# A hybrid attention and RWKV layer on one core: the values' channel sum pinned behind the solve

## The chip, the cores and the metric

The kernel runs on one core of a Trainium2 chip. The metric is device time in microseconds, from one launch; of the kernel before there are three timed runs, and one more that was recorded by the profiler. A difference is a change of the median of such runs.

Engines are named as in the profile: PE (matrix), DVE (vector), ACT (scalar), POOL (GpSimd), SP (the queue that issues nearly all DMAs). PEld is PE's loading of stationary operands.

## The reference

One layer, 256 tokens of width 4096, all in float32. One projection of the input feeds 16 heads of attention with forget gates (width 128) and 32 heads of RWKV-7 time mixing (width 64); their outputs are gated, projected and normalised:

```
proj = x @ w_in                                   # fox q,k,v,f | rwkv r,k,v,w,a | gate z
fox  = softmax(q k^T / sqrt(128) + forget decay) v   # causal, per head
rw   = rw + (previous token's rw - rw) * mu       # token shift of r, k, v, w, a
S_t  = S_{t-1} diag(w_t) + (S_{t-1} a_t) b_t^T + v_t k_t^T ;  y_t = S_t r_t
y    = GroupNorm per head(y) + sum(r k r_k) v
out  = LayerNorm(ALPHA * x + (concat(fox, y) * silu(z)) @ w_out)
```

The GroupNorm subtracts each head's mean over its 64 channels. The kernel uses that y is linear in v: it subtracts the mean from the values v, once, before the recurrence. That is the centring of which the change speaks, and the sum over channels is its first step.

## The kernel before

**The main stream.** The projection's weights come in tiles of 512 KB, each holding two of the 32 blocks of 128 input channels by 512 columns. A column block takes 16 such tiles, numbered 0 to 15 (in the profile w_0 to w_15); four column blocks b = 0 to 3 make one pass n, and there are eight passes, one for each pair n of head tiles (128 channels each, two RWKV heads or one attention head). Every tile is split in two halves for float32 accuracy: ACT casts it (line 138, tile w_7h for instance) and DVE subtracts the cast (line 139, w_7l). PE takes three products with them (lines 144 to 146; line 146 is the one that needs the DVE half), four times for each tile. Buffers: four raw tiles, four cast halves, three DVE halves. Then the output projection streams its own tiles in the same way (names wo, lines 784 to 786).

**The side work.** Everything else is done by generators that advance by one step in each `slot()`, two slots for each weight tile. `W` and `LAG` say how many slots each waits between its steps. `chain()` runs `rwkv(n)` for the eight pairs, and around the change it does this, with the block and tile of the stream beside which it stands:

- Block 2: PE multiplies keys and queries of all chunks into four PSUM tiles gp (line 488). POOL turns the values of the pair, which were written to memory and read back one token later (tile vs), into the shifted values: lines 493, 494, 495. POOL also scales the kept keys BK (line 491), once PE has read them. DVE masks gp into gb and lt (lines 506 and 514, eight instructions of 64x512); SP stores parts of gb (line 509) and loads them back in another layout, Nb (line 510).
- Block 2's end to block 3's tile 7: a triangular system is solved by back substitution on DVE, 31 steps of a product (line 536) and a sum (line 539), one step in each slot.
- Behind it, SP stores the solution xc (line 545) and loads it back as T (line 547). DVE sums the values over channels, vm (line 550); eight DVE instructions subtract the mean and write SV (line 557); ACT copies each of the two SV tiles to UV (line 560). Twelve slots later the transposes of T follow (line 566), and the chunk recurrence.

**What sets the order.** The kernel's text is a program order, and a scheduler may place an instruction on its engine ahead of others that it doesn't depend on, when it finds it ready earlier. `tc.keep_in_program_order(...)` takes that freedom from an instruction: it stays behind what stands ahead of it in the text. Lines 537 and 566 pin the solve's first product and the transposes. Line 550 isn't pinned: in the text it stands behind the solve, on DVE it stood in block 2. Each engine takes its instructions strictly in its own order, and waits at the first one that isn't ready.

Of the kernel before, what the change touches and what calls it, by code (L numbers as in the profile page):

```python
# [14 lines left out]
ALU = mybir.AluOpType  # L15
AX = mybir.AxisListType
# [8 lines left out]
HD = 64  # L25
# [57 lines left out]
def layer(ctx: ExitStack, tc: tile.TileContext, xt, xtok, w_lora, w_main, muv, w_o, up, par, mulora, fbias, lng, lnb, cst, out):  # L83
    nc = tc.nc
# [292 lines left out]
    vs_ = {}  # L377
# [98 lines left out]
    def rwkv(n):  # L476
# [12 lines left out]
        v = vv[n]  # L489
        kept = BK[:, :, 0 : NCH - 1, :]  # L490
        nc.gpsimd.tensor_tensor(kept, kept, lc[:, :, 0 : NCH - 1].unsqueeze(3).to_broadcast([P, 2, NCH - 1, P]), ALU.mult)
        p, t = bks[n], vs_[n]
# [54 lines left out]
                nc.sync.dma_start(out=T[B * a : B * (a + 1), u], in_=td[u, a].rearrange("c r s -> r c s"))  # L547
        vm = rp.tile([P, 2, 2, 2], F32, tag="vm", name=f"vm{n}")
        vt = vs_[n].rearrange("p m (u j v) -> p m u j v", u=2, j=2)
        nc.vector.tensor_reduce(vm.rearrange("p m u j -> p (m u j)"), vs_[n].rearrange("p m (a v) -> p (m a) v", v=HD), AX.X, ALU.add)  # L550
        yield
        for j in range(2):
            o = HALF[1 - j]
# [14 lines left out]
        for u in range(2):  # L568
            for c in range(NCH):
                for j in range(2):  # L570
                    a, b = slice(C * j, C * j + B), slice(C * j + B, C * j + C)
# [17 lines left out]
        for u in range(2):  # L589
            for c in range(NCH):  # L590
                for j in range(2):
                    a, b = slice(C * j, C * j + B), slice(C * j + B, C * j + C)
                    nc.tensor.matmul(xp[a, u * P + c * B : u * P + (c + 1) * B], Q[b, u, c, :], X[b, u, c, C * j + B : C * j + C], start=True, stop=True)
        for j in range(2):
            a = slice(C * j, C * j + B)
# [110 lines left out]
    def chain():  # L706
        while not ff:
            yield
        yield from forget()
        for n in range(G // 2):  # L710
            yield from rwkv(n)
# [304 lines left out]
```

## Time and profile before

| what | us |
|---|---|
| timed runs | 1991.75, 1997.97, 1998.69 |
| median | 1997.97 |
| profiled execution, its own time | 1994.46 |
| its span, first to last instruction | 1992.7 |
| PE busy in the span | 1967.0 |
| DVE busy | 1356.3 |
| ACT busy | 999.1 |
| POOL busy | 72.6 |

A row of the timeline has the start, the length, engine, line, operation, the tiles written and read, shapes, how many instructions were merged, and in brackets the idle time of the engine before it with what ended it. A row of the waits has who waited for whom, the total in us, how many times, and the longest. A row of the stretches has its length, the busy time of PE, PEld, DVE, ACT and POOL with the number of instructions, the clock that was granted to PE as a share of the full one, the share of time in which the DMA engines were busy, and GB/s. Matmuls overlap, so a row's length is longer than the spacing from one to the next.

### The profile page before, as it was taken

What the parts mean: (1) busy time and instruction counts of PE and PEld (TensorE: products, weight loads), DVE (VectorE), ACT (ScalarE), POOL (GpSimd) and SP (SyncE); (2) the same over time, 40 slices, a digit from 0 to 9 for tenths busy, and PEclk for the clock granted to TensorE, in tenths of its full rate; (3) what the DMA queues carried; (4) which work ended last, traced back from release to release, by engine and by line L of the source; (5) the groups of instructions that cost most, each with busy time, mean ns of one, the idle gap of its engine ahead of it and who ended that gap; (6) DMA issues with size and microseconds to landing.
All of it is one profiled execution on the core that took longest, in us unless ns stands there. A gap on an engine that the chain in (4) does not pass through costs nothing. (4 is left out here: it accounts for less than half of the span.)

```text
span 1992.7 us, 28327 instructions
## 1 busy us (share of the span) xinstructions
PE 1967.0 (99%) x10377; PEld 1611.1 (81%) x10377; DVE 1356.3 (68%) x2168; ACT 999.1 (50%) x1509; POOL 72.6 (4%) x111
## 2 busy tenths in 40 slices
PE   9999999999999999999999999999999999999998
PEld 7878787878787878787878787877888878888886
DVE  6688577857685767577857785768577856755555
ACT  6554564456445644464446444644465444443332
POOL 0110001000100010001000100010001000000000
PEclk9999999999999999999999999999999999999999
DMA  9556556655666566555655565556555877866664
GB/s 334 159 176 195 182 190 187 198 180 188 179 203 179 191 180 200 181 183 181 206 180 183 182 207 173 191 173 206 182 189 172 266 271 228 256 199 201 195 189 170
DMA packets 146383, 392.86 MB, mean 197 GB/s; under 512 B 32642, under 2 KB 48020, under 8 KB 146244
## 3 DMA queue, kind: packets, MB, share of 16 engines
q1 hardware_dynamic: 145812, 390.63, 62.6%
q8 instruction: 81, 1.33, 0.3%
q14 instruction: 58, 0.48, 0.1%
q10 hardware_dynamic: 432, 0.43, 0.1%
HBM read 374.98 MB, written 16.01 MB: 196 GB/s over the span
## 5 line engine op out<-in xcount | busy, mean ns | idle before, releaser
L138 ACT CAST w_11h<-w 128x1024 fp32r<-128x1024 f32 x31 | 32.6, 1051 | 91.0 <-DMA w<-in_w_main_dram 72.2
L536 DVE TENSOR_TENSOR prod<-Nb,xc 128x8 f32<-128x8 f32 (+30 forms) x248 | 72.5, 292 | 7.1
L539 DVE TENSOR_REDUCE xc<-prod 128x8 f32<-128x16 f32 (+30 forms) x248 | 73.2, 295 | 6.0
L139 DVE TENSOR_TENSOR w_11l<-w,w_11h 128x1024 fp32r<-128x1024 f32 x31 | 37.9, 1223 | 47.0 <-ACT w_11h L138 28.7
L146 PE MATMUL acc<-w_7l,x 128*128 128x512 f32 x124 | 51.8, 418 | 15.4 <-DVE w_7l L139 15.4
L139 DVE TENSOR_TENSOR w_1l<-w,w_1h 128x1024 fp32r<-128x1024 f32 x31 | 37.9, 1224 | 35.7 <-PE acc L146 35.7
L139 DVE TENSOR_TENSOR w_0l<-w,w_0h 128x1024 fp32r<-128x1024 f32 x31 | 37.9, 1224 | 34.0 <-PE acc L146 23.8
L139 DVE TENSOR_TENSOR w_3l<-w,w_3h 128x1024 fp32r<-128x1024 f32 x31 | 37.8, 1221 | 31.8 <-PE acc L146 31.8
L138 ACT CAST w_2h<-w 128x1024 fp32r<-128x1024 f32 x31 | 32.7, 1056 | 52.2 <-PE acc L145 46.8
L138 ACT CAST w_1h<-w 128x1024 fp32r<-128x1024 f32 x31 | 32.7, 1055 | 51.6 <-PE acc L145 42.0
L138 ACT CAST w_0h<-w 128x1024 fp32r<-128x1024 f32 x31 | 32.7, 1056 | 43.5 <-PE acc L145 34.1
L139 DVE TENSOR_TENSOR w_10l<-w,w_10h 128x1024 fp32r<-128x1024 f32 x31 | 38.0, 1225 | 23.6 <-PE acc L146 13.8
L139 DVE TENSOR_TENSOR w_9l<-w,w_9h 128x1024 fp32r<-128x1024 f32 x31 | 37.9, 1224 | 23.0 <-ACT pT L688 19.2
L139 DVE TENSOR_TENSOR w_2l<-w,w_2h 128x1024 fp32r<-128x1024 f32 x31 | 37.9, 1223 | 22.6 <-PE acc L146 22.4
L139 DVE TENSOR_TENSOR w_15l<-w,w_15h 128x1024 fp32r<-128x1024 f32 x31 | 37.9, 1222 | 22.3 <-PE acc L146 20.9
L138 ACT CAST w_13h<-w 128x1024 fp32r<-128x1024 f32 x31 | 32.6, 1053 | 40.7 <-DMA w<-in_w_main_dram 23.8
L144 PE MATMUL acc<-w_4h,x 128*128 128x512 f32 x124 | 53.0, 427 | 0.0
L144 PE MATMUL acc<-w_7h,x 128*128 128x512 f32 x124 | 51.6, 416 | 0.0
L138 ACT CAST w_4h<-w 128x1024 fp32r<-128x1024 f32 x31 | 32.7, 1055 | 36.8 <-PE acc L145 35.5
L144 PE MATMUL acc<-w_6h,x 128*128 128x512 f32 x124 | 51.2, 413 | 0.0
L144 PE MATMUL acc<-w_1h,x 128*128 128x512 f32 x124 | 51.2, 413 | 0.0
L144 PE MATMUL acc<-w_2h,x 128*128 128x512 f32 x124 | 51.1, 412 | 0.0
(836 smaller groups left out, 6582.0 us busy)
## 6 DMA issues: line engine op xcount, KB each, us to landing
w<-in_w_main_dram SPq DMA_DIRECT2D x496, 512.0 KB, 3.5
wo<-in_w_o_dram SPq DMA_DIRECT2D x128, 512.0 KB, 3.6
Nb<-nd SPq DMA_DIRECT2D x16, 512.0 KB, 5.3
wr<-in_w_main_dram SPq DMA_DIRECT2D x15, 512.0 KB, 6.8
hd<-hl SPq DMA_DIRECT2D x29, 256.0 KB, 4.4
h<-hd SPq DMA_DIRECT2D x29, 256.0 KB, 6.6
res<-in_xtok_dram SPq DMA_DIRECT2D x16, 256.0 KB, 4.5
xr<-in_xt_dram SPq DMA_DIRECT2D x15, 256.0 KB, 6.4
```

Of the source, the lines that this page charges most:

```text
L138: nc.scalar.copy(hi[:, :n], src[:, :n])
L139: nc.vector.tensor_tensor(lo[:, :n], src[:, :n], hi[:, :n].bitcast(F32), ALU.subtract)
L144: nc.tensor.matmul(acc[:, :n], xs[k][:, 0, tt], hi[:, o : o + n], start=(k == 0), stop=False)
L146: nc.tensor.matmul(acc[:, :n], xs[k][:, 0, tt], lo[:, o : o + n], start=False, stop=(k == KT - 1))
L536: first = nc.vector.tensor_tensor(prod[:, :, :, s + 1 :], nb[:, :, s : s + 1, s + 1 :].to_broadcast([P, 2, NJ, w]), xc[:, :, :, s + 1 :], ...
L539: nc.vector.tensor_reduce(xc[:, :, :, s : s + 1], prod[:, :, :, s:], AX.X, ALU.add)
```

## The change

Line 550, the sum over the values' channels, is put into `keep_in_program_order`:

```
-        nc.vector.tensor_reduce(vm.rearrange("p m u j -> p (m u j)"), vs_[n].rearrange("p m (a v) -> p (m a) v", v=HD), AX.X, ALU.add)
+        tc.keep_in_program_order(nc.vector.tensor_reduce(vm.rearrange("p m u j -> p (m u j)"), vs_[n].rearrange("p m (a v) -> p (m a) v", v=HD), AX.X, ALU.add))
```

No instruction is added or taken away. The order on PE, POOL and SP is the same; on DVE and ACT three groups move in each of the eight passes. On DVE in block 2 of pair 2, ahead of the masks (vm is the sum, SV_2 the centred values, w_2_5l the DVE half of tile 5 of block 2, gb_838 the first masked tile):

```order
 L266 SCALAR_TENSOR_TENSOR s_4_4972<-tr_1_0_4967,prm,s_4_4972 128x255
 L517 TENSOR_TENSOR bon_4585<-bon_4585,s_4_4972 128x512
-L550 TENSOR_REDUCE vm_5627<-vs_4930 128x8
 L139 TENSOR_TENSOR w_2_5l<-w_2_5_5001,w_2_5h 128x1024
-L557 SCALAR_TENSOR_TENSOR SV_2_5075<-vm_5627,vs_4930 64x2x64 x4
-L557 SCALAR_TENSOR_TENSOR SV_2_5076<-vm_5627,vs_4930 64x2x64 x4
 L139 TENSOR_TENSOR w_2_6l<-w_2_6_5019,w_2_6h 128x1024
 L506 TENSOR_TENSOR gb_838<-gp_0_0_5031,cs 64x512
```

The sum and the eight instructions of the centring have left this place; between the bonus term (line 517) and the masks only the splits of tiles 5 and 6 remain.

On DVE in block 3 of the same pair, at the end of the solve (prod and xc are its last step):

```order
 L536 TENSOR_TENSOR prod_5203<-Nb_5056,xc_5204 128x8x31
 L539 TENSOR_REDUCE xc_5204<-prod_5203 128x8
+L550 TENSOR_REDUCE vm_5627<-vs_4930 128x8
 L139 TENSOR_TENSOR w_3_8l<-w_3_8_5512,w_3_8h 128x1024
+L557 SCALAR_TENSOR_TENSOR SV_2_5075<-vm_5627,vs_4930 64x2x64 x4
+L557 SCALAR_TENSOR_TENSOR SV_2_5076<-vm_5627,vs_4930 64x2x64 x4
 L139 TENSOR_TENSOR w_3_9l<-w_3_9_5540,w_3_9h 128x1024
 L139 TENSOR_TENSOR w_3_10l<-w_3_10_5573,w_3_10h 128x1024
```

They now stand behind the solve's last sum, around the split of tile 8 and ahead of that of tile 9.

On ACT in block 3 of the same pair (UV_2 are the copies of the centred values, pT an attention tile):

```order
 L138 CAST w_3_9h<-w_3_9_5540 128x1024
 L688 COPY pT_5530<-fpt_5526 128x384
+L560 COPY UV_2_5077<-SV_2_5075 64x512
 L138 CAST w_3_10h<-w_3_10_5573 128x1024
+L560 COPY UV_2_5078<-SV_2_5076 64x512
 L138 CAST w_3_11h<-w_3_11_5595 128x1024
 L695 COPY fo_5565<-fop_5562 128x256
```

The two copies followed the centring: from block 2, where they stood around the cast of tile 7, to block 3, around the cast of tile 10.

## The prediction

> **What bounds the kernel now.** I read the page's head first, then what PE waited for, and only then the stretch of one pair of heads in the timeline.
>
> ```profile
> span 1992.7 us, 28327 instructions
> ...
> PE 1967.0 (99%) x10377; PEld 1611.1 (81%) x10377; DVE 1356.3 (68%) x2168; ACT 999.1 (50%) x1509; POOL 72.6 (4%) x111
> ```
>
> PE is the bound: 1967.0 of 1992.7 us. An edit on DVE can only pay by what PE loses to DVE. Of the rows on PE's waits one matters:
>
> ```profile
> PE acc L146 <- DVE w_7l L139: 15.4, 8, 2.1
> ```
>
> Eight waits, one for each pair of heads, all for the same tile: the low half of weight tile 7 in column block 2. The timeline of pair 2 shows why it is late (DVE, then POOL, ACT and PE; columns: start, length):
>
> ```profile
> 530.93 0.69 DVE L550 TENSOR_REDUCE vm<-vs 128x8 f32<-128x512 f32 x1 [4.07 <-POOL vs L495]
> 531.53 1.22 DVE L139 TENSOR_TENSOR w_5l<-w,w_5h 128x1024 fp32r<-128x1024 f32 x1
> 532.78 3.21 DVE L557 SCALAR_TENSOR_TENSOR SV<-vm,vs 64x128 f32<-64x128 f32 x8
> 536.02 1.23 DVE L139 TENSOR_TENSOR w_6l<-w,w_6h 128x1024 fp32r<-128x1024 f32 x1
> 537.17 1.40 DVE L506 TENSOR_TENSOR gb<-gp,cs 64x512 f32<-64x512 f32 x2
> ...
> 542.66 1.21 DVE L139 TENSOR_TENSOR w_7l<-w,w_7h 128x1024 fp32r<-128x1024 f32 x1
> ...
> 533.15 1.47 POOL L491 TENSOR_TENSOR BK<-BK,lc 128x768 f32<-128x768 f32 x1 [2.25 <-PE gp L488]
> ...
> 530.38 1.04 ACT L138 CAST w_6h<-w 128x1024 fp32r<-128x1024 f32 x1
> ...
> 531.22 2.06 PE L488 MATMUL gp<-lt,BK 64*128 64x128 f32 x32
> ...
> 541.18 0.39 PE L144 MATMUL acc<-w_7h,x 128*128 128x512 f32 x1
> 541.41 0.40 PE L145 MATMUL acc<-w_7h,x 128*128 128x512 f32 x1
> 543.92 0.61 PE L146 MATMUL acc<-w_7l,x 128*128 128x512 f32 x1 [2.12 <-DVE w_7l L139]
> ```
>
> DVE stands idle for 4.07 us until POOL has finished the shifted values, takes the sum over channels (L550), the centring (L557), two weight splits, and comes to the eight masks at 537.17, although PE had finished their input at 531.22 + 2.06 = 533.28. The masks run until the split of tile 7 starts at 542.66, which is 5.49 us; the split ends at 543.87 and PE starts at 543.92.
>
> PE loses more than the listed wait. The clock that the throttle granted, in stretches of 3.41 us (columns: length, PE, PEld, DVE, ACT, POOL, clock, DMA share, GB/s):
>
> ```profile
> 144.80:148.21 3.41, 3.41 (x9) 2.63 (x9) 1.98 (x2) 0.00 (x0) 0.00 (x0) 0.50 1.02 245
> 544.16:547.57 3.41, 3.41 (x9) 2.63 (x9) 1.98 (x2) 0.00 (x0) 0.00 (x0) 0.50 0.76 202
> 745.55:748.96 3.41, 3.41 (x10) 2.63 (x9) 1.66 (x3) 0.00 (x0) 0.00 (x0) 0.50 1.00 214
> 1144.91:1148.32 3.41, 3.29 (x8) 2.63 (x9) 2.33 (x3) 0.00 (x0) 0.00 (x0) 0.50 1.05 244
> 344.38:347.79 3.41, 3.41 (x15) 2.81 (x16) 2.95 (x3) 0.00 (x0) 0.00 (x0) 1.00 1.01 237
> 540.75:544.16 3.41, 1.29 (x6) 0.77 (x5) 3.38 (x5) 1.05 (x1) 0.00 (x0) 1.00 0.17 24
> ```
>
> In four of these stretches the clock is 0.50; pair 2's starts at 544.16, right behind the stall that ended at 543.92, and the stretch before it had PE busy for 1.29 of 3.41 us. The other three begin behind the stalls of pairs 0, 3 and 5, and behind pair 1's shorter stall the clock stayed at 1.00. I take it that a stall falling mostly into one such stretch halves the clock for the next.
>
> **What is removed.** Three terms, each eight times or fewer:
> - The listed wait of PE: 15.4 us.
> - Refilling: 541.18 to 541.41 is the regular spacing, 0.23 us; 541.41 to 543.92 is 2.51, so 2.28 is lost where 2.12 is listed. The 0.16 us, eight times: 1.3 us.
> - Half clock: half of 3.41 us in each of four stretches: 4 x 1.7 = 6.8 us.
>
> Sum: 23.5 us. The profiled execution took 1994.46 us (its span and 1.8 us around it), so 1971.0 us, on a span of 1969.2. The median of the three timed runs is 3.5 us above the profiled one; two more half-clock stretches would make that difference (an estimate from the row above, not seen). If it were something else, the sum from the median would be 1974.5. I keep 1971.0, because the changed kernel should have no such stretches left to vary.
>
> **Does the wait go entirely?** In pair 2 the split of tile 6 can start when its ACT half is there, 530.38 + 1.04 = 531.42, and ends at 532.65. The masks then wait for PE until 533.28 at the latest, run 5.49 us to 538.77, and the split of tile 7 ends at 539.98. PE wants it one spacing after 541.41, at 541.64: 1.66 us to spare. The masks now run beside POOL's L491 (1.47 us), which they don't before, and DVE operations do stretch beside POOL:
>
> ```profile
> L557 DVE SCALAR_TENSOR_TENSOR SV<-vm,vs x64: 275/284/1605, 133.1 to 1537.4; 64x128 f32<-64x128 f32 x64
> ```
>
> The median is 0.284 us and the longest 1.605, so the bound for that is 1.605 - 0.284 = 1.32 us, which still leaves 0.34 of the 1.66. The nearer row is that of another operation with one input in PSUM and one in SBUF, as the masks have:
>
> ```profile
> 124.73 0.48 DVE L266 SCALAR_TENSOR_TENSOR s<-tr,prm,s 128x255 f32<-128x255 f32 x1
> ...
> 126.13 0.48 DVE L266 SCALAR_TENSOR_TENSOR s<-tr,prm,s 128x255 f32<-128x255 f32 x1
> ...
> 125.99 1.29 POOL L493 TENSOR_TENSOR vs<-vs,bk 128x512 f32<-128x512 f32 x1 [18.40 <-DMA vs<-vd]
> ```
>
> The second of these runs wholly inside POOL's operation and takes the same 0.48 us. I take zero. A gain beyond the sum is excluded here, since the PE wait can't go below nothing.
>
> **What is added.** The sum, the centring and its two ACT copies now stand in column block 3, behind the solve's last reduce. Pair 2 there, before:
>
> ```profile
> 588.68 0.42 DVE L539 TENSOR_REDUCE xc<-prod 128x8 f32<-128x256 f32 x1
> 589.02 1.22 DVE L139 TENSOR_TENSOR w_8l<-w,w_8h 128x1024 fp32r<-128x1024 f32 x1
> 590.98 1.23 DVE L139 TENSOR_TENSOR w_9l<-w,w_9h 128x1024 fp32r<-128x1024 f32 x1 [0.75 <-issue]
> ...
> 597.31 0.39 PE L146 MATMUL acc<-w_9l,x 128*128 128x512 f32 x1
> ```
>
> New on DVE: 0.69 (L550) + 8 x 0.284 (L557) = 2.96 us ahead of the split of tile 9. Its values have long been ready, so L550 waits for nobody. Of the 2.96 us the idle 0.75 takes the first part; the split then starts at 593.19 and ends at 594.42, and PE wants it at 597.31: 2.9 us to spare. Nothing reaches PE. On ACT the first copy of the centred values (L560) waits for four of the eight pieces, until 589.10 + 0.69 + 1.22 + 4 x 0.284 = 592.15; the casts of tiles 10 and 11 stand behind the two copies. With a copy (64x512 values) at half a cast's 1.04 us (an estimate), tile 10's cast ends near 593.7, ahead of its DVE split, which follows 594.42 anyway. The attention copy and the gate behind them come about 1 us later, which DVE's idle time before tiles 11 and 12 takes up. The solve's result still goes out on SP directly behind L539; L550 stands behind that instruction on DVE, so the round trip through memory isn't held. SP, POOL and PE keep their order. The masks' stores are issued earlier, so the solve's input and the weights behind them on SP come no later than now. I take all this at zero; from below it can't gain, since PE doesn't wait in this place, and from above rival 3 prices it.
>
> [...]
>
> **The rivals.**
> 1. The half-clock stretches are not caused by the stalls and stay. Then only 15.4 + 1.3 go: 1977.8 us. For it: not each stall is followed by one. Against it: all four follow a stall. Chance 0.07.
> 2. Tile 7 stays late, by half: the masks are delayed beside POOL by more than 1.66 us a pair, or start later than PE allows. Half of the 23.5 us remains: 1982.7 us. Against it are the 1.66 us to spare. Chance 0.06.
> 3. Slower: the centring stalls PE at tile 9 of block 3. It decides once the added DVE work is longer than 0.75 + (597.31 - 592.21) = 5.85 us. If each of the eight L557 took the 1.605 us of the longest, the work would be 13.5 us, the stall 7.7 us a pair, 61 us for eight, less the 23.5 gained: 2032 us. It needs 8.8 us of work to end slower than now. Against it: the long ones stand beside POOL's work, and in this place POOL has had none for 70 us when its next begins:
>
> ```profile
> 604.70 0.29 POOL L669 TENSOR_SCALAR_AFFINE_SELECT nb<-nb 128x128 f32<-128x128 f32 x1 [70.08 <-DMA nb<-ncd]
> ```
>
> Chance 0.04.
> 4. Another wait takes the whole place of the removed one (weight tiles 10 or 11 arriving behind the solve's input): about 1994 us. For it: PE now arrives there up to 2 us sooner. Against it: the loads are released sooner too. Chance 0.08.
>
> **How the numbers follow.** The forecast has the remaining 0.75. Its own spread is 1967 to 1975: upward by the 3.5 us between profiled run and median, downward as much. The range leaves out rivals 3 and 4, 12 in 100, and takes in 1 and 2 whole; below it gets 2 us more for what else a chip may differ by: 1965 to 1983. A difference of 0.5% is some 10 us, about what a measurement of this kernel can tell from no change. Faster by more: forecast and rivals 1 and 2, 0.88; I move 0.02 of it to no change, since rival 2 reaches to there. Faster 0.86, same 0.10, slower 0.04.
>
> **What would show it.** In the profile after, the row of PE waiting for tile 7 is gone; no stretch in mid-run has clock 0.50; DVE's L550 has no idle time before it; L557 has a longest near 0.29 us; the masks of pair 2 start as soon as PE has filled gp; and the splits of tiles 9 to 12 in block 3 still end ahead of PE. The forecast is wrong if PE's row of waits names another tile with over 1 us a pair, or if stretches at 0.50 are still there without stalls before them.

## The result, and the profile after

The changed kernel takes 1968.84 us in the median of four runs (1967.9 to 1969.22), against 1995.62 us before (four runs, 1991.75 to 1998.69: the three named above and one of 1993.26): a ratio of 0.9866, with a 95% interval from 0.9845 to 0.9887. The forecast was 1971.0, in a range from 1965 to 1983.

The page of the changed kernel, from the execution that took 1967.9 us; its span, and the chain that ended last, by engine:

```profile
span 1966.1 us, 28320 instructions
...
PE 98%; DVE 1%; ACT 0%; issue 0%; ACTq 0%; DVEq 0%
```

The chain can now be followed along PE for almost the whole span. What PE waited for, the whole list (total, times, longest):

```profile
PE zp L921 <- DVE zd L909: 1.4, 1, 1.4
PE warmup L106 <- POOL idle L103: 1.3, 1, 1.3
PE fpt L686 <- DVE lg L682: 0.3, 1, 0.3
PE wp L933 <- ACT l L923: 0.2, 1, 0.2
PE accl L144 <- ACT wl0h L138: 0.2, 1, 0.2
```

The row of 15.4 us for tile 7 is gone, and no other has come in its place: what is left are waits at the start and the end, and one of 0.3 us. The stretch from 100 to 1900 us, first before, then after (length, PE, PEld, DVE, ACT, POOL, clock, DMA share, GB/s):

```profile
100.00:1900.00 1800.00, 1783.67 (x9485) 1460.20 (x9484) 1238.25 (x1980) 906.15 (x1354) 66.84 (x96) 1.00 0.63 195
```

```profile
100.00:1900.00 1800.00, 1799.71 (x9602) 1478.49 (x9601) 1245.20 (x1990) 916.85 (x1364) 74.94 (x96) 1.00 0.66 198
```

PE is busy for 1799.71 of 1800 us, and gets through 9602 matmuls where it was 9485. The rows give the clock to two digits only; in the clock records of the changed kernel it is full from 7.3 to 1963.1 us. The first place, pair 2 in block 2 (DVE, then POOL, then PE):

```profile
526.48 1.23 DVE L139 TENSOR_TENSOR w_6l<-w,w_6h 128x1024 fp32r<-128x1024 f32 x1 [3.06 <-ACT w_6h L138]
527.62 1.40 DVE L506 TENSOR_TENSOR gb<-gp,cs 64x512 f32<-64x512 f32 x2
528.94 0.69 DVE L514 TENSOR_TENSOR lt<-gp,cs 64x512 f32<-64x512 f32 x1
...
533.11 1.21 DVE L139 TENSOR_TENSOR w_7l<-w,w_7h 128x1024 fp32r<-128x1024 f32 x1
...
527.47 1.56 POOL L491 TENSOR_TENSOR BK<-BK,lc 128x768 f32<-128x768 f32 x1 [1.54 <-PE gp L488]
...
525.55 2.06 PE L488 MATMUL gp<-lt,BK 64*128 64x128 f32 x32
...
535.85 0.39 PE L146 MATMUL acc<-w_7l,x 128*128 128x512 f32 x1
```

The masks start at 527.62, when PE has just finished gp (525.55 + 2.06 = 527.61); before, they started 3.9 us behind it. Tile 7's split ends at 534.32, 1.5 us ahead of the matmul that needs it. The second place, pair 2 in block 3:

```profile
580.07 0.42 DVE L539 TENSOR_REDUCE xc<-prod 128x8 f32<-128x256 f32 x1
580.41 0.68 DVE L550 TENSOR_REDUCE vm<-vs 128x8 f32<-128x512 f32 x1
581.00 1.22 DVE L139 TENSOR_TENSOR w_8l<-w,w_8h 128x1024 fp32r<-128x1024 f32 x1
582.25 2.02 DVE L557 SCALAR_TENSOR_TENSOR SV<-vm,vs 64x128 f32<-64x128 f32 x8
584.30 1.23 DVE L139 TENSOR_TENSOR w_9l<-w,w_9h 128x1024 fp32r<-128x1024 f32 x1
...
588.03 0.39 PE L146 MATMUL acc<-w_9l,x 128*128 128x512 f32 x1
```

The sum starts at once, the centring takes 2.02 us where it took 3.21, and tile 9's split ends at 585.53, 2.5 us ahead of PE.

### The profile page after: what moved, and what is told of

The parts are those of the page before. It is cut to its first block, busy times and chain, and to the rows that moved or that the text cites. A ratio compares the mean times of both kernels' runs of the same rounds, so it can differ in the third digit from the quotient of the medians.

```text
span 1966.1 us, 28320 instructions
## 1 busy us (share of the span) xinstructions
PE 1955.8 (99%) x10377; PEld 1608.1 (82%) x10377; DVE 1351.5 (69%) x2168; ACT 999.5 (51%) x1509; POOL 81.0 (4%) x111
## 4 chain that ended last, share of the span: by engine, by line
PE 98%; DVE 1%; ACT 0%; issue 0%; ACTq 0%; DVEq 0%
PE acc L144 24%; PE acc L146 24%; PE acc L145 24%; PE oacc L784 6%; PE oacc L786 6%; PE oacc L785 6%; PE tr L735 1%; PE yp L634 1%; PE gp L488 1%; PE up L609 1%; PE rh L582 1%; PE sp L618 0%; PE accl L146 0%; PE accl L144 0%; PE accl L145 0%; PE tp L525 0%
## 5 line engine op out<-in xcount | busy, mean ns | idle before, releaser
L139 DVE TENSOR_TENSOR w_6l<-w,w_6h 128x1024 fp32r<-128x1024 f32 x31 | 38.0, 1226 | 37.0 <-ACT w_6h L138 17.5
L139 DVE TENSOR_TENSOR w_14l<-w,w_14h 128x1024 fp32r<-128x1024 f32 x31 | 38.0, 1225 | 19.7 <-PE acc L146 9.0
L139 DVE TENSOR_TENSOR w_5l<-w,w_5h 128x1024 fp32r<-128x1024 f32 x31 | 43.5, 1403 | 10.9 <-PE acc L146 10.9
```

The source lines that it names most:

```text
L139: nc.vector.tensor_tensor(lo[:, :n], src[:, :n], hi[:, :n].bitcast(F32), ALU.subtract)
```

## The experiments

The theory: what counts is how long DVE works ahead of the masks, since tile 7's split stands behind them; the time comes back as PE's waits and as half-clock stretches that those waits bring on. Two rivals: that the sum's wait for POOL is the cause, and that the half-clock stretches have nothing to do with the stalls.

**The centring pinned, the sum left free.** Against the kernel before:

```
-                    nc.vector.scalar_tensor_tensor(
+                    tc.keep_in_program_order(nc.vector.scalar_tensor_tensor(
                         SV[j][o, :, 2 * a + c, :], vm[h, a, :, j].unsqueeze(2).to_broadcast([C, 2, HD]), -1.0 / HD, vt[h, a, :, j, :], ALU.mult, ALU.add
-                    )
+                    ))
```

> The kernel before, with the eight centring instructions (line 557) pinned and the sum (line 550) left free: the sum and its wait for POOL stay in front of the masks, the centring goes to block 3. Theory (the length of what stands on DVE in front of the masks makes tile 7 late): in pair 2 the sum ends at 531.6, tiles 5 and 6 are split by 533.9, the masks run to 539.4, tile 7's split ends at 540.6 where PE wants it at 541.64; no PE wait for tile 7, no half-clock stretch in mid-run, 1969 us, the same as the changed kernel within 0.3%. Rival (the wait for POOL in front of the sum is the cause): the PE waits stay, 1985 us or more.

Measured: 1970.44 us, ratio to before 0.9868 (0.9854 to 0.9883), the same as the changed kernel. The sum is still in front and DVE still stands idle for POOL, as DVE in pair 2 shows:

```profile
526.07 0.69 DVE L550 TENSOR_REDUCE vm<-vs 128x8 f32<-128x512 f32 x1 [3.92 <-POOL vs L495]
...
528.94 1.40 DVE L506 TENSOR_TENSOR gb<-gp,cs 64x512 f32<-64x512 f32 x2
```

Of PE's waits for tile 7 one is left, 0.7 us in the last pair:

```profile
PE acc L146 <- DVE w_7l L139: 0.7, 1, 0.7
```

So the rival falls: an idle 3.92 us ahead of the masks costs almost nothing by itself, because the masks can't start before PE has finished gp. In pair 2 they start 0.4 us behind gp; only in the last pair, where they start 2.4 us behind it, does PE wait. It is the centring behind the wait for POOL that made tile 7 late. (The centring stands even later here, ahead of tile 13 of block 3, and PE doesn't wait for that tile; its smaller waits, for lg and Q, are 1.2 us longer in all than in the changed kernel.)

**Stalls of chosen length.** Four kernels repeat DVE's split of tile 7 of block 2, k more times, with the same result (here k = 2). The rest of the text is the changed kernel's, but the scheduler orders DVE anew around the repeats, and with three and four of them it also lets PE take two matmuls ahead of the waiting one:

```
-        nc.vector.tensor_tensor(lo[:, :n], src[:, :n], hi[:, :n].bitcast(F32), ALU.subtract)
+        for _ in range(3 if name.endswith("_2_7") else 1): nc.vector.tensor_tensor(lo[:, :n], src[:, :n], hi[:, :n].bitcast(F32), ALU.subtract)
```

Two more:

> The changed kernel, with DVE's split of tile 7 of block 2 done twice more in each pass (same result, 2.26 us longer). Theory: PE has 0.7 to 1.5 us to spare there, so it stalls 0.7 to 1.6 us a pair, about 8 us in all, and 2 us for refilling; a stall this short leaves no stretch of 3.41 us with PE mostly idle, so the clock is never halved in mid-run: 1979 us. Rival (half-clock stretches come with any stall, or at random): some stretches at 0.50 in mid-run, 1.7 us each, up to 1990 us.

Three more:

> The same with three repeats (3.4 us longer; the scheduler takes two matmuls ahead of the waiting one, 0.5 us). Theory: stalls of 1.5 to 2.2 us a pair, 15 us, 2 us for refilling, and those stalls of over 1.8 us that fall into one stretch halve the clock for the next: two or three stretches of 1.7 us each, 1990 us, and the runs of this kernel differ among each other by several us. [...]

Four more:

> The same with four repeats (4.5 us longer). Theory: stalls of 2.6 to 3.3 us a pair, 24 us, 2 us for refilling, and five to seven half-clock stretches of 1.7 us: 2004 us. [...]

Once more, designed after these three:

> The changed kernel, with DVE's split of tile 7 of block 2 done once more in each pass; the scheduler puts the split of tile 8 between the two, so the tile is ready 2.26 us later. PE has 0.7 to 1.5 us to spare there, so the stalls are 0.7 to 1.6 us a pair. Theory (a stretch of 3.41 us halves the clock of the next only when PE stands idle in it for more than some 1.8 us): no stretch at 0.50 in mid-run; about 8 us of stalls and 0.35 us a pair for refilling, 1980 us. Rival (any stall can halve the clock): one to four stretches at 0.50, 1982 to 1987 us.

The first three expectations missed the times, by 10, 22 and 24 us: 1989.14, 2012.05 and 2027.82 us were measured (ratios to before 0.9961, 1.0079 and 1.0158). With two repeats it was the rival that described what came, some half-clock stretches and up to 1990 us; with three and four repeats 9 and 14 of them came, where two or three and five to seven were expected. I had overlooked that the scheduler puts the split of tile 8 between the repeats, which adds another 1.1 us to each stall, and with the longer stalls came more half-clock stretches, 3, 9 and 14. The stalls can be read, though. PE's waits for tile 7 with one, two, three and four repeats:

```profile
PE acc L146 <- DVE w_7l L139: 5.6, 7, 1.1
```

```profile
PE acc L146 <- DVE w_7l L139: 13.3, 8, 2.4
```

```profile
PE acc L146 <- DVE w_7l L139: 25.9, 8, 4.0
```

```profile
PE acc L146 <- DVE w_7l L139: 38.9, 8, 5.3
```

With one repeat no stall is longer than 1.1 us, and the clock stays full from 5.9 us to 1965 us, as expected and against the rival. That kernel took 1973.39 us (ratio to before 0.9878), 6.6 us less than expected, because the stalls came to 5.6 us in place of 8. Its profiled execution is the longest of the four, 1975.22, which is 7.3 us above the changed kernel's 1967.9, and 5.6 us of waits with some 0.25 us for refilling in seven pairs make 7.4. (The medians, with other executions in them, are 4.6 us apart.)

With two repeats, where no wait is longer than 2.4 us, three stretches ran at half clock, and other stalls had none behind them. PE's clock in pairs of stretches of 3.41 us, one with the stall in it and the next (the first columns are the length and PE's busy time; the clock is third from the end):

```profile
341.59:345.00 3.41, 1.52 (x7) 0.90 (x7) 3.38 (x4) 1.05 (x1) 0.00 (x0) 1.00 1.03 234
345.00:348.41 3.41, 3.41 (x10) 2.64 (x9) 0.48 (x1) 0.22 (x1) 0.00 (x0) 0.50 1.00 364
542.97:546.39 3.42, 1.00 (x4) 0.86 (x5) 3.39 (x3) 0.39 (x1) 0.00 (x0) 1.00 1.04 240
546.39:549.80 3.41, 3.41 (x9) 2.67 (x8) 0.58 (x2) 0.45 (x1) 0.00 (x0) 0.50 1.01 317
...
1539.66:1543.08 3.42, 1.79 (x8) 1.50 (x9) 2.68 (x3) 0.00 (x0) 0.00 (x0) 1.00 1.00 271
1543.08:1546.49 3.41, 3.41 (x17) 2.83 (x16) 1.23 (x1) 1.06 (x1) 0.00 (x0) 1.00 0.99 330
```

Where PE was busy for 1.52 and 1.00 us of a stretch, the next ran at half clock (a third such pair, with 1.53 us, is left out); where it was busy for 1.79 us, it ran at full clock. The stall before 1541.29 was longer (2.08 us) than the one before 344.39 (1.89 us), and yet only the shorter was followed by half clock: the longer one fell across two stretches. These half-clock stretches begin a whole multiple of 3.413 us apart (345.00 and 546.39 are 59 of them apart, 546.39 and 1143.72 are 175). With four repeats six of the eight stalls were followed by two such stretches, and the clock is at half over both:

```profile
553.98:560.81 6.83, 5.52 (x13) 4.36 (x14) 2.45 (x2) 1.05 (x1) 0.00 (x0) 0.50 0.64 199
```

The same sum fits two repeats: 1967.9 us of the changed kernel, 13.3 us of listed waits, 3 x 1.7 us at half clock and 8 x 0.3 us for refilling make 1988.7; the profiled execution took 1989.67. With three and four repeats it comes out too high, 2011.5 with 9 half-clock stretches and 2033.0 with 14, where the profiled executions took 2009.95 and 2027.36: in part of those stretches PE was still waiting (9.1 us in all with four repeats), and half clock cost nothing there.

**More work in the new place.** The same repeat for tile 9 of block 3, twice more (the scheduler also moved one weight load on SP in each pass):

```
-        nc.vector.tensor_tensor(lo[:, :n], src[:, :n], hi[:, :n].bitcast(F32), ALU.subtract)
+        for _ in range(3 if name.endswith("_3_9") else 1): nc.vector.tensor_tensor(lo[:, :n], src[:, :n], hi[:, :n].bitcast(F32), ALU.subtract)
```

> The changed kernel, with DVE's split of tile 9 of block 3, right behind the moved centring, done twice more in each pass (2.26 us longer). Theory: PE has 2.5 to 3.8 us to spare for this tile in the profile of the changed kernel, so nothing reaches PE: 1969 us, the same within 0.3%, no PE wait for tile 9. Rival (the new place is as tight as the old one): PE waits for tile 9 in most pairs, 1975 us or more.

Measured: 1969.13 us, ratio to before 0.9856 (0.9842 to 0.9871), and no PE wait for tile 9. In pair 2 three splits stand behind the centring, and PE still comes later:

```profile
581.22 2.02 DVE L557 SCALAR_TENSOR_TENSOR SV<-vm,vs 64x128 f32<-64x128 f32 x8
583.27 3.74 DVE L139 TENSOR_TENSOR w_9l<-w,w_9h 128x1024 fp32r<-128x1024 f32 x3
...
587.64 0.39 PE L146 MATMUL acc<-w_9l,x 128*128 128x512 f32 x1
```

They end at 587.01, and 0.6 us are left, the least of the eight pairs. The new place takes the moved work and nearly as much again.

No kernel tried here is faster than the changed one by more than can be measured.

## Why the prediction was right, step by step

**The listed wait, 15.4 us: right.** It went entirely, and nothing took its place. The spare time at tile 7 in pair 2 was forecast as 1.66 us and is 1.5 us. But this margin was worked out for one pair alone: over the eight it runs from 0.7 us (pair 4, where the masks wait for the split of tile 6 and start 0.8 us behind gp) to 2.4 us.

**The half clock, 6.8 us: right.** In mid-run no stretch of the changed kernel is at 0.50, and the repeats show that the stalls bring such stretches on: none with stalls of at most 1.1 us, 3, 9 and 14 with two, three and four repeats. Rival 1, that they are unrelated and stay, is refuted. The size holds too. In pair 2, from the stalled matmul to the ninth behind it, PE took 3.75 us before (543.92 to 547.67) and 2.05 us after (535.85 to 537.90), so half clock cost 1.70 us; counted in the same way it cost 1.71, 1.72 and 1.64 us in pairs 0, 3 and 5, 6.8 us in all. This term was the step that rested most on a guess, since the trace of before had four stretches only; the repeats also show with what it went that not each stall had one, PE's busy time in the stretch before (1.52 us against 1.79). One reading was not exact: the half-clock stretch of pair 5 doesn't begin behind its stall, it begins at 1144.91, 0.1 us before the stall ends at 1145.03. Of the stretch before, from 1141.50, PE was busy for 1.40 us.

**Refilling, 1.3 us: a little too small, and two waits left out.** Profile against profile the kernel gained 1994.46 - 1967.9 = 26.6 us, 3.1 more than the sum of 23.5. PE reaches gp of the first pair at the same time in both (132.32 and 132.28 us), and the readout of the last pair 26.4 us earlier, as its rows show, before and after:

```profile
1625.43 0.29 PE L634 MATMUL yp<-lt,SV 128*64 128x64 f32 x4
```

```profile
1599.07 0.29 PE L634 MATMUL yp<-lt,SV 128*64 128x64 f32 x4
```

So the missing 3 us lie in the eight pairs, not at the ends. For pair 4 of before, whose clock stayed full:

```profile
942.83 0.39 PE L145 MATMUL acc<-w_7h,x 128*128 128x512 f32 x1
945.34 0.50 PE L146 MATMUL acc<-w_7l,x 128*128 128x512 f32 x1 [2.12 <-DVE w_7l L139]
945.68 0.40 PE L144 MATMUL acc<-w_7h,x 128*128 128x512 f32 x1
```

The matmul behind the first one is late as well: 0.34 us of spacing where 0.23 is regular. With it, refilling is 2.28 + 0.11 - 2.12 = 0.27 us in such a pair, where I took 0.16. In the four pairs with half clock the second late matmul is already within the 6.8 us, so this accounts for 0.4 of the 3.1 us.

Another part was in PE's list of waits before, where I had said that one row matters:

```profile
PE tp L525 <- DVE lt L514: 0.4, 1, 0.4
PE acc L146 <- DVE w_6l L139: 0.3, 1, 0.3
```

Both waits are in pair 6, where DVE had waited longest for POOL (5.14 us) and came to the masks 4.9 us behind gp, so that PE also waited for tile 6 and for a masked tile. From the matmul at 1339.46 to the one at 1342.55 PE took 3.09 us; for the same matmuls it takes 1.93 after (1319.13 to 1321.06). These 1.2 us went with the rest, and the forecast had put them at nothing. Where the last 1.5 us went, less than 0.2 us a pair, stays open.

**The masks beside POOL, taken as zero: right.** In the changed kernel they run beside L491, and the pair of them takes 1.40 us as before. The row of L266 was the right neighbour, and rival 2 with its bound of 1.32 us from L557 is out.

**The new place, taken as zero: right.** In pair 2 the spare time at tile 9 was forecast as 2.9 us and is 2.5 us, the least of the eight pairs. An ACT copy, estimated at half a cast or 0.52 us, takes 0.62 us (L560), and PE waits for nothing behind it. L557 is free of POOL there, as its row in the changed kernel shows (shortest, median, longest in ns):

```profile
L557 DVE SCALAR_TENSOR_TENSOR SV<-vm,vs x64: 276/284/290, 187.1 to 1566.0; 64x128 f32<-64x128 f32 x64
```

Rival 3 needed the long form of it, which didn't appear: before, there was one in each pair, 1444 to 1605 ns, and all eight ran beside L491. Rival 4, another wait in the same place, didn't come about: PE's list names no tile of the main stream (wl0h is a tile at the very start).

**The base.** I took the profiled run rather than the median, expecting the changed kernel to vary less. Its four runs lie within 1.3 us, where those of before lie within 6.9. That half-clock stretches make up the difference between the runs of before is likely, but isn't shown: of the later runs of before the longest (2001.18 us) had the lowest mean clock, 0.993, and the shortest (1994.71 us) the highest, 0.998, but those between don't follow that order.

## What to carry to other kernels

Where an engine feeds the one that bounds the kernel and takes its instructions in order, look at what it does ahead of the urgent instruction and needs only later. DVE did so here: before, the split of tile 5 in pair 2 had its ACT half at 525.56 and its buffer at 527.22, and started at 531.53, behind the sum that waited for POOL until 530.93. The 3 us of sum and centring, needed only some 85 us later, cost 3.3 us for each pair of heads on average. A scheduler that takes what is ready first doesn't know that. And count a short stall of PE with what follows it: in pair 2 the listed 2.12 us cost 3.98, 2.28 with refilling and 1.70 at half clock.

## What the runs showed of the hardware

In the kernel before, PE's clock was at 0.50 in four stretches of 3.41 us in mid-run, from 144.80, 544.16, 745.55 and 1144.91 us. These starts are 117, 59 and 117 times 3.413 us apart. The stalls ahead of them ended between 0.92 us earlier (744.63) and 0.12 us later (1145.03).

With the time cut into such stretches from these starts on, PE's busy time in the one ahead, at full clock, was 1.59, 1.29, 1.30 and 1.40 us where half clock followed; in the other four pairs the stretch with most of the stall had 2.15, 1.60, 1.74 and 2.10 us, and full clock followed. With two repeats it was 1.52, 1.00 and 1.53 us ahead of half clock, and 1.94 and 1.79 us ahead of full clock in the two other pairs read. In the kernel before the two cases meet at 1.6 us, too close for these rows, in which the ends of matmuls are modelled, to tell apart:

```profile
141.39:144.80 3.41, 1.59 (x7) 1.01 (x7) 3.38 (x5) 1.25 (x2) 0.00 (x0) 1.00 0.14 19
144.80:148.21 3.41, 3.41 (x9) 2.63 (x9) 1.98 (x2) 0.00 (x0) 0.00 (x0) 0.50 1.02 245
943.52:946.94 3.42, 1.60 (x7) 1.32 (x8) 3.42 (x4) 0.09 (x1) 0.00 (x0) 1.00 0.72 175
946.94:950.35 3.41, 3.41 (x17) 2.80 (x16) 1.84 (x2) 0.00 (x0) 0.00 (x0) 1.00 0.96 244
```

By the length of the stall: none of the seven with one repeat, of at most 1.1 us, was followed by half clock. Before, those of 1.82, 2.12, 2.11 and 2.13 us were, and those of 1.26, 2.12, 2.14 and 1.71 us weren't. All sixteen of 2.8 us or more, with three and four repeats, were followed by it. A half-clock stretch of the kernel before cost 1.64 to 1.72 us.

Behind a stretch that was itself at half clock, 2.41 us of busy PE were followed by half clock again with four repeats, and 3.26 us by full clock with three:

```profile
1168.38:1171.79 3.41, 2.41 (x6) 1.93 (x7) 0.95 (x1) 0.00 (x0) 0.00 (x0) 0.50 0.75 231
1171.79:1175.21 3.42, 3.42 (x10) 2.65 (x9) 1.23 (x1) 1.05 (x1) 0.00 (x0) 0.50 0.15 61
```

```profile
549.91:553.33 3.42, 3.26 (x8) 2.59 (x9) 0.10 (x1) 0.00 (x0) 0.00 (x0) 0.50 1.00 321
553.33:556.74 3.41, 3.41 (x17) 2.78 (x16) 1.44 (x2) 1.50 (x2) 0.00 (x0) 1.00 0.40 106
```

So the stall that reached 1.00 us into the half-clock stretch behind it was followed by a second one, and the one that reached 0.15 us into it wasn't. No run here shows what follows between 2.41 and 3.26 us.
